# A hybrid attention and state-space block on one core: one z granule earlier, the merge started a quarter earlier, two norms rearranged

## The chip, the cores and the metric

The kernel runs on one core of a Trainium2 chip. The core's engines run side by side, each with its own in-order queue: TensorE (PE, with PEld for its weight loads), VectorE (DVE), ScalarE (ACT), GpSimd (POOL) and SyncE (SP), which here only issues transfers. The metric is the device time of one execution in microseconds, the median of several; lower is better.

## The reference, cut to what matters

One decoder block, 256 positions, width 2048, all float32. An attention branch with a top-64 choice of keys for each query and a state-space (SSD) branch run on the same modulated input; they are merged by gates, projected, added to the residual, and a SwiGLU feed-forward part with a second norm and a final norm follow.

```python
h = rms_norm(x, norm1_g[l]) * (1.0 + sc1) + sh1
proj = h @ w_in            # split: c_q, c_kv, k_idx, w_idx, z, xbc, dt, g_a, g_b
y_a = dsa_branch(...)      # idx_score -> top_k -> 16 heads of attention on the chosen keys
y_b = ssd_branch(z, xbc, ...)          # conv, chunked scan, * silu(z), group rms_norm
merged = sigmoid(g_a) * (y_a @ w_proj_a) + sigmoid(g_b) * (y_b @ w_proj_b)
x = x + g1 * (merged @ w_out)
h = rms_norm(x, norm2_g[l]) * (1.0 + sc2) + sh2
x = x + g2 * ((silu(h @ w_gate) * (h @ w_up)) @ w_down)
return rms_norm(x, final_g)
```

## The kernel before, in words

**Layout.** Activations are kept transposed, 128 channels on the partitions by 256 positions; a product granule is one 128x2048 piece of weights, that is 16 tiles of 128x128. Each granule is a `Job`. SP loads the raw piece (1 MB); `split` turns it into a high part `wh` (ACT, L178) and a low part `wl` (DVE, L179); the job's function then issues the matmuls. Activations are split in the same way into 512 columns (high, low). A product of one tile is two matmuls where the accumulator is 512 wide (`wide`: 512 columns for the high weights, 256 for the low, L202 and L203), and three of 256 columns where it is not (L205 to L207). When an accumulator is full, its `post` is put off to the start of the next job (`flush`).

**Order.** `run_jobs` goes through the list of jobs: it runs the posts put off, then splits the weights of the job two places ahead (`process_to`), then runs the job's `pre` hook, then its function. Generators (index scores and top-k, heads, SSD) advance one step for each tick of a job. All this is the order in which instructions are traced; a planner then lays out each engine's queue by this priority and by modelled readiness, so an instruction of lower priority can fill a modelled gap. Background entries (`add_bg`) are pieces of the modulation matrix that DVE multiplies and adds up (L424, L426).

**Stages.** First the small projections and the modulation (to about 300 us); 8 z granules, during which the 8 steps of index scores and then the top-k run on DVE (L638, L639); 8 pairs of heads with a z granule after each; 4 z granules; 16 granules of proj_a (`add_pa`); 48 granules of the convolution input mixed with the last z granules and the first half of proj_b; the second half of proj_b; 16 granules of the output projection (`add_out`); gate and up; down; the final norm.

**A head** (`head_gen`): logits on PE (L749, L750), bias plus mask on POOL (L753, L754), softmax on DVE and ACT (L759 to L766), transposes on PE (L770).

**The merge.** proj_b sums over 32 tiles in four quarters q of 8 granules, each granule two output rows m; `pb` in SBUF holds the sum (L1007). In the last quarter `merge_load` fetches the stored gates `sg` and the stored attention part `sa` for each m, and `merge` multiplies by the gate on DVE (L1038), adds `sa` on POOL (L1039) and splits the result into `mg` (ACT L250, DVE L251). The first granule of the output projection reads `mg` row by row.

**The second norm** (`norm2`, the `pre` of the first gate granule): the squares of 15 rows are summed on POOL, the last row's square stays apart; `rms_rows` sums over the partitions on PE (L301), takes the square root (L293) and the reciprocal (L294), and spreads the result over the partitions on PE (L312); then for each of 16 rows DVE, ACT and DVE make `h2` (L1087 to L1089). **The final norm** does the same, ACT copies the factor to SBUF (L1250), and DVE and POOL multiply the 16 rows (L1254), stored in 9 transfers (L1255) from the SP and ACT queues.

## Time and profile before

| what | value |
|---|---|
| median of 3 runs | 2051.14 us (2050.96 to 2054.85) |
| the profiled execution | 2048.58 us |
| its span, first to last instruction | 2046.9 us |
| busy: PE, DVE, ACT, POOL | 1999.2, 1460.8, 1049.9, 185.0 us |
| mean granted PE clock | 0.987 of full |

PE is busy for 98% of the span. [...] Times in a timeline are microseconds from the span's start.

### The profile page before, as it was taken

To read this page: it belongs to the slowest core of one execution; us is meant where nothing else is said; L and a number is where in the kernel's file an instruction comes from. 1 tells how busy PE (TensorE), PEld (TensorE's weight loads), DVE (VectorE), ACT (ScalarE), POOL (GpSimd) and SP (SyncE) were. 2 spreads that over 40 slices of the span, in tenths; PEclk is the share of its full clock that TensorE was granted. 3 is DMA by queue.
4 is the path that set the end of the run, shared out by engine and by line. 5 is a ranking of instruction groups with operands and counts; after the bars stand their busy time and mean duration, and the time that the engine had idled before them with its cause. 6 is when DMAs were issued, how large, how long until landed. Compare 5 with 4: busy or idle time off the path is not lost.

```text
span 2046.9 us, 31681 instructions
## 1 busy us (share of the span) xinstructions
PE 1999.2 (98%) x12888; PEld 1786.3 (87%) x12888; DVE 1460.8 (71%) x1819; ACT 1049.9 (51%) x1427; POOL 185.0 (9%) x160
## 2 busy tenths in 40 slices
PE   8999999999999999999999999999999999999997
PEld 6899998899888888889989988888888888888886
DVE  6777787977678888888787855667776555544443
ACT  4655474565346766667664434544444444443432
POOL 0000000220000111110112344000000000000000
PEclk8999999999999999999999999999999999999998
DMA  9887776666887767766666676457775555565552
GB/s 372 330 308 294 277 253 242 232 220 229 292 319 282 252 249 254 260 229 242 224 247 217 235 264 212 164 208 292 264 297 197 188 187 187 200 217 187 187 185 83
DMA packets 100033, 490.17 MB, mean 239 GB/s; under 512 B 10512, under 2 KB 43648, under 8 KB 46384
## 3 DMA queue, kind: packets, MB, share of 16 engines
q1 hardware_dynamic: 98224, 484.10, 65.6%
q0 software_dynamic: 704, 3.15, 0.4%
q8 instruction: 101, 1.65, 0.3%
q10 hardware_dynamic: 960, 0.92, 0.1%
q14 instruction: 44, 0.36, 0.0%
HBM read 473.35 MB, written 17.92 MB: 240 GB/s over the span
## 4 chain that ended last, share of the span: by engine, by line
PE 85%; issue 7%; DVE 4%; ACT 3%; POOL 1%; DMA 1%; DVEq 0%; POOLq 0%; ACTq 0%
PE acc_gu L202 15%; PE acc_dn L202 8%; PE acc_cv L202 8%; PE acc_gu L203 8%; PE acc_dn L203 4%; PE acc_cv L203 4%; PE acc_z L202 4%; PE acc_pa L202 3%; PE acc_out L202 3%; PE cyc L706 2%; PE cyc L704 2%; PE cyc L705 2%; PE acc_pb L205 2%; PE acc_pb L206 2%; PE acc_pb L207 2%
## 5 line engine op out<-in xcount | busy, mean ns | idle before, releaser
L179 DVE TENSOR_TENSOR wl<-raw,wh 128x2048 fp32r<-128x2048 f32 (+1 forms) x316 | 722.1, 2286 | 356.5 <-ACT wh L178 355.8
L178 ACT ACTIVATE wh<-raw 128x2048 fp32r<-128x2048 f32 (+1 forms) x316 | 599.1, 1897 | 371.8 <-PE acc_dn L202 99.8
L202 PE MATMUL acc_gu<-h,wh 128*128 128x512 f32 x1312 | 459.6, 396 | 0.0
L203 PE MATMUL acc_gu<-h,wl 128*128 128x256 f32 x1312 | 367.2, 280 | 0.0
L202 PEld LDWEIGHTS acc_gu<-h,wh 128*128 128x128 f32 x1312 | 246.1, 188 | 58.3
L202 PE MATMUL acc_cv<-h,wh 128*128 128x512 f32 x768 | 277.6, 403 | 0.0
L202 PE MATMUL acc_dn<-ffact,wh 128*128 128x512 f32 x704 | 248.8, 396 | 0.0
L203 PEld LDWEIGHTS acc_gu<-h,wl 128*128 128x128 f32 x1312 | 247.6, 189 | 0.0
L203 PE MATMUL acc_cv<-h,wl 128*128 128x256 f32 x768 | 215.6, 281 | 0.0
L203 PE MATMUL acc_dn<-ffact,wl 128*128 128x256 f32 x704 | 198.5, 282 | 0.0
L202 PE MATMUL acc_z<-h,wh 128*128 128x512 f32 x512 | 183.4, 400 | 0.0
L202 PEld LDWEIGHTS acc_cv<-h,wh 128*128 128x128 f32 x768 | 144.1, 188 | 37.4 <-issue 4.7
L426 DVE SCALAR_TENSOR_TENSOR acc<-raw,cact,acc 128x1024 f32<-128x1024 f32 x120 | 158.5, 1321 | 5.2 <-DMA raw<-in_ada_dram 4.7
L202 PEld LDWEIGHTS acc_dn<-ffact,wh 128*128 128x128 f32 x704 | 132.3, 188 | 32.3
L704 PE MATMUL cyc<-h,wh 128*128 128x256 f32 x512 | 147.9, 289 | 5.1 <-ACT cyc L679 1.8
L706 PE MATMUL cyc<-h,wl 128*128 128x256 f32 x512 | 144.8, 288 | 3.1 <-DVE wl L179 3.1
L705 PE MATMUL cyc<-h,wh 128*128 128x256 f32 x512 | 146.4, 286 | 0.0
L203 PEld LDWEIGHTS acc_cv<-h,wl 128*128 128x128 f32 x768 | 145.1, 189 | 1.0 <-issue 0.5
L205 PE MATMUL acc_pb<-y,wh 128*128 128x256 f32 x512 | 145.1, 283 | 0.0
L203 PE MATMUL acc_z<-h,wl 128*128 128x256 f32 x512 | 143.4, 280 | 0.0
L206 PE MATMUL acc_pb<-y,wh 128*128 128x256 f32 x512 | 142.6, 279 | 0.0
L207 PE MATMUL acc_pb<-y,wl 128*128 128x256 f32 x512 | 142.5, 278 | 0.0
(311 smaller groups left out, 3606.2 us busy)
## 6 DMA issues: line engine op xcount, KB each, us to landing
raw<-in_w_gu_dram SPq DMA_DIRECT2D x88, 1024.0 KB, 4.7
raw<-in_ada_dram SPq DMA_DIRECT2D x75, 1024.0 KB, 5.0
raw<-in_w_ssm_dram SPq DMA_DIRECT2D x48, 1024.0 KB, 4.9
raw<-in_w_dn_dram SPq DMA_DIRECT2D x44, 1024.0 KB, 4.7
raw<-in_w_z_dram SPq DMA_DIRECT2D x32, 1024.0 KB, 5.0
raw<-in_w_pb_dram SPq DMA_DIRECT2D x32, 1024.0 KB, 4.8
raw<-in_w_s_dram SPq DMA_DIRECT2D x27, 1024.0 KB, 6.8
raw<-in_w_pa_dram SPq DMA_DIRECT2D x16, 1024.0 KB, 5.3
```

Source lines behind the costliest of these rows:

```text
L178: act.activation(whf[:, o], raw[:, o], AF.Copy)
L179: dve.tensor_tensor(wlf[:, o], raw[:, o], whf[:, o].bitcast(F32), op=ALU.subtract)
L202: pe.matmul(acc, wh, rhs, start=first, stop=last)
L203: pe.matmul(acc[:, :L], wl, rhs[:, :L], start=False, stop=last, skip_group_check=True)
L205: pe.matmul(acc, wh, rhs[:, :L], start=first, stop=False)
L206: pe.matmul(acc, wh, rhs[:, L:], start=False, stop=False)
L207: pe.matmul(acc, wl, rhs[:, :L], start=False, stop=last)
L426: dve.scalar_tensor_tensor(a, r, cact[:, k : k + 1], a, op0=ALU.mult, op1=ALU.add)
L704: pe.matmul(acc, wh[:, t], h[:, k, :L], start=first, stop=False, skip_group_check=True)
L705: pe.matmul(acc, wh[:, t], h[:, k, L:], start=False, stop=False, skip_group_check=True)
L706: pe.matmul(acc, wl[:, t], h[:, k, :L], start=False, stop=(c == n - 1), skip_group_check=True)
```

## The change

A ninth z granule stands ahead of the first pair of heads, and three instead of four follow the last pair (`ZLEAD`). In the third quarter of proj_b (q = 2) the sum so far is already multiplied by the gate and `sa` is added (`merge_most`); in the last quarter the gate, loaded a second time, multiplies the accumulator and the product is added on DVE, with no POOL step. The last row of the output projection and of down uses a 256-column accumulator (`narrow`), so its post is one DVE instruction. `rms_cols` sums the early squares of both halves first, then the last row's. `norm2` is traced ahead of the split of the weights two places ahead (`first`), with four matmuls ahead of the column sums and four behind the spread whose results nobody reads. At the end DVE multiplies with the factor out of PSUM, POOL with the copy in SBUF; the rows are dealt out anew, POOL's four in two pieces.

```diff
+ZLEAD = 9
-OUTC = ((0, 1), (1, 2), (2, 3), (3, 5), (12, 16), (5, 7), (7, 9), (9, 11), (11, 12))
+OUTC = ((0, 1), (1, 2), (2, 4), (12, 14), (4, 6), (6, 8), (14, 16), (8, 10), (10, 12))
+OUTP = 12
@@ run_jobs
+            if job.first and job.pre:
+                job.pre()
             process_to(jobs[min(i + AHEAD, len(jobs) - 1)].entry)
-            if job.pre:
+            if job.pre and not job.first:
                 job.pre()
@@ product_jobs
-                        if not wide:
+                        if not wide or m in narrow:
                             accs[key, m] = accs[key, m][:, :L]
@@ rms_cols
-        for c in range(2):
-            for i, s in enumerate(sums):
+        for i, s in enumerate(sums):
+            for c in range(2):
                 pe.matmul(
-                    ps[:, c : c + 1], s[:, c * P : c * P + P], ones[:, 0:1], start=(i == 0), stop=(i == len(sums) - 1)
+                    ps[:, c : c + 1], s[:, c * P : c * P + P], ones[:, 0:1],
+                    start=(i == 0 and c == 0), stop=(i == len(sums) - 1), skip_group_check=True,
                 )
@@ add_pb
-            dve.tensor_tensor(pb, acc, pb, op=ALU.add)
-            if q == 3:
-                merge(m, pb)
+            if q < 3:
+                dve.tensor_tensor(pb, acc, pb, op=ALU.add)
+                if q == 2:
+                    merge_most(m, pb)
+            else:
+                merge(m, pb, acc)
@@
-        product_jobs(..., pref=merge_load if q == 3 else None)
+        product_jobs(..., pref=merge_load if q >= 2 else None)
@@ merge_load, merge
         sg = tmp.tile([P, L], F32, tag="zv", name="sgr")
+        nc.sync.dma_start(sg, d_sgb[m])
+        Cc["ld", m] = sg
+
+    def merge_most(m, pb):
+
         sa = tmp.tile([P, L], F32, tag="zt", name="sar")
-        nc.sync.dma_start(sg, d_sgb[m])
         nc.sync.dma_start(sa, d_sa[m])
-        Cc["ld", m] = sg, sa
-
-    def merge(m, pb):
-        sg, sa = Cc.pop(("ld", m))
-        dve.scalar_tensor_tensor(pb, sg, 1.0, pb, op0=ALU.add, op1=ALU.mult)
+        dve.scalar_tensor_tensor(pb, Cc.pop(("ld", m)), 1.0, pb, op0=ALU.add, op1=ALU.mult)
         pool.tensor_tensor(pb, pb, sa, op=ALU.add)
+
+    def merge(m, pb, acc):
+        sg = Cc.pop(("ld", m))
+        dve.scalar_tensor_tensor(sg, sg, 1.0, acc, op0=ALU.add, op1=ALU.mult)
+        dve.tensor_tensor(pb, pb, sg, op=ALU.add)
         split_act(pb, Cc["mg"][:, m])
@@ add_out (add_down alike)
-            dve.scalar_tensor_tensor(x1, acc[:, L:], mods[:, 0, m : m + 1], x1, op0=ALU.mult, op1=ALU.add)
+            if acc.shape[1] > L:
+                dve.scalar_tensor_tensor(x1, acc[:, L:], mods[:, 0, m : m + 1], x1, op0=ALU.mult, op1=ALU.add)
...
+        product_jobs(..., pref=pref, wide=True, narrow=(15,))
@@ norm2
-        r = rms_rows([Cc["acc"], Cc["last"]], D, "n2")
+        dummy = ps_side("busy")
+        for _ in range(4):
+            pe.matmul(dummy[:, :L], ones, Cc["acc"], start=True, stop=True)
+        r = rms_cols([Cc["acc"], Cc["last"]], D, "n2")
+        rp, r = r, rms_all(r, "n2")
+        for _ in range(4):
+            pe.matmul(dummy[:, :L], rp[:, 0:1].to_broadcast([P, P]), Cc["last"], start=True, stop=True)
@@ the list of jobs
-    sp = Spread(8, BG[0])
-    for i in range(8):
+    sp = Spread(ZLEAD, BG[0])
+    for i in range(ZLEAD):
         add_z(next(zs))
...
-    sp = Spread(20, BG[1])
+    sp = Spread(28 - ZLEAD, BG[1])
...
-    for _ in range(4):
+    for _ in range(12 - ZLEAD):
         add_z(next(zs))
@@ the end
-        eng = pool if b == 16 else dve
+        eng, f = (pool, r) if a >= OUTP else (dve, rp)
         v = Fd["x2"][:, a:b]
-        eng.tensor_tensor(v, v, r[:, None, :].to_broadcast([P, b - a, L]), op=ALU.mult)
+        eng.tensor_tensor(v, v, f[:, None, :].to_broadcast([P, b - a, L]), op=ALU.mult)
```

## Rows read from the trace of the kernel before

**Rows 1.** The page's first part: busy time, share of the span and instructions of each engine.

```profile
PE 1999.2 (98%) x12888; PEld 1786.3 (87%) x12888; DVE 1460.8 (71%) x1819; ACT 1049.9 (51%) x1427; POOL 185.0 (9%) x160
```

**Rows 2.** The view of waits of engine PE over the whole span: who waited for whom, us in total, times, longest.

```profile
PE pT L770 <- DVE part L766: 5.0, 3, 2.3
...
PE acc_out L202 <- DVE mg L251: 4.0, 2, 3.4
```

**Rows 3.** The first heads. First two stretches of the view of windows (length, then busy time and count of PE, PEld, DVE, ACT, POOL, then the granted PE clock, DMA share, GB/s); then the timeline of PE and of DVE (start, duration, engine, line, operation, count, and in brackets the idle time before it and its releaser).

```profile
359.00:377.00 18.00, 18.00 (x134) 16.82 (x132) 17.96 (x61) 9.52 (x15) 1.08 (x4) 1.00 0.42 162
...
388.20:394.70 6.50, 4.18 (x21) 3.89 (x20) 6.46 (x14) 3.27 (x12) 0.52 (x1) 0.50 0.75 286
...
384.52 0.28 PE L203 MATMUL acc_z<-h,wl 128*128 128x256 f32 x1
...
391.19 0.69 PE L770 MATMUL pT<-ident,part 128*128 128x128 f32 x2 [2.32 <-DVE part L766]
...
374.11 2.30 DVE L179 TENSOR_TENSOR wl<-raw,wh 128x2048 fp32r<-128x2048 f32 x1
...
390.79 0.34 DVE L766 TENSOR_SCALAR part<-part,mx 128x256 f32<-128x256 f32 x1
```

**Rows 4.** The end of the merge and the first granule of the output projection: timeline of PE, one window as above, timeline of DVE and of SP (its transfers' issues).

```profile
1182.44 0.40 PE L202 MATMUL acc_out<-mg,wh 128*128 128x512 f32 x1
...
1191.82 0.79 PE L202 MATMUL acc_out<-mg,wh 128*128 128x512 f32 x1 [3.38 <-DVE mg L251]
...
1191.80:1196.40 4.60, 4.58 (x14) 3.90 (x15) 1.69 (x4) 1.82 (x2) 0.73 (x1) 0.50 0.79 267
...
1181.57 0.43 DVE L1038 SCALAR_TENSOR_TENSOR pbacc<-sgr,pbacc 128x256 f32<-128x256 f32 x1 [1.80 <-DMA sgr<-d_sgb]
...
1191.35 0.42 DVE L251 TENSOR_TENSOR mg<-pbacc,mg 128x256 fp32r<-128x256 f32 x1
...
1174.54 0.33 SPq L1032 DMA_DIRECT2D sgr<-d_sgb  x1
```

**Rows 5.** The third and the last quarter of proj_b, roughly, in the view of windows; and from the view of the tile y (1100 to 1140 us) the last part of the split of the last SSD group: duration min/median/max, first and last start.

```profile
1092.00:1137.00 45.00, 45.00 (x394) 43.29 (x393) 31.98 (x41) 18.68 (x19) 8.40 (x8) 1.00 0.58 208
1137.00:1182.00 45.00, 43.50 (x371) 43.32 (x370) 38.45 (x52) 17.68 (x19) 21.33 (x12) 1.00 0.74 265
...
L251 DVE TENSOR_TENSOR y<-xc,y x4: 418/420/426, 1131.8 to 1133.8; 128x256 fp32r<-128x256 f32 x4
```

**Rows 6.** Timeline of PE: two instructions 16 tiles (one granule) apart in the output projection, two one tile apart in proj_b.

```profile
1262.22 0.39 PE L202 MATMUL acc_out<-mg,wh 128*128 128x512 f32 x1
...
1267.80 0.40 PE L202 MATMUL acc_out<-mg,wh 128*128 128x512 f32 x1
...
1176.44 0.28 PE L205 MATMUL acc_pb<-y,wh 128*128 128x256 f32 x1
...
1176.79 0.28 PE L205 MATMUL acc_pb<-y,wh 128*128 128x256 f32 x1
```

**Rows 7.** The second norm: timeline of PE, of DVE and of ACT; the last row is a float32 matmul of 256 columns (two passes) in the heads.

```profile
1278.61 0.28 PE L301 MATMUL n<-ones,ssq 128*128 128x1 f32 x2
...
1282.63 1.22 PE L312 MATMUL n2b<-ident,rcol 128*128 128x128 f32 x4 [0.55 <-DVE rcol L294]
1285.69 0.76 PE L202 MATMUL acc_g<-h,wh 128*128 128x512 f32 x1 [1.84 <-DVE h L1089]
...
1289.00 0.40 PE L202 MATMUL acc_g<-h,wh 128*128 128x512 f32 x1
...
1279.97 0.48 DVE L1071 SCALAR_TENSOR_TENSOR pbacc<-acc_out,mods,pbacc 128x256 f32<-128x256 f32 x1
...
1280.79 0.40 ACT L1046 ACTIVATE sqs<-pbacc 128x256 f32<-128x256 f32 x1
...
380.77 0.60 PE L750 MATMUL lg<-part 128*128 128x256 f32 x2
```

**Rows 8.** The final norm: timeline of DVE, PE, ACT, POOL and SP, and from the view of transfers (2030 to 2047 us, 40 slices of 0.425 us) what they moved.

```profile
2032.39 0.48 DVE L1148 SCALAR_TENSOR_TENSOR x<-acc_dn,mods,x 128x256 f32<-128x256 f32 x1 [12.44 <-PE acc_dn L203]
...
2034.20 0.36 PE L301 MATMUL nf<-ones,x 128*128 128x1 f32 x2
2034.42 0.36 PE L301 MATMUL nf<-ones,sqs 128*128 128x1 f32 x2
2035.33 0.71 PE L312 MATMUL nfb<-ident,rcol 128*128 128x128 f32 x4 [0.55 <-DVE rcol L294]
...
2036.08 0.38 ACT L1250 ACTIVATE x<-nfb 128x256 f32<-128x256 f32 x1 [1.00 <-PE nfb L312]
...
2036.84 2.56 DVE L1254 TENSOR_TENSOR x<-x 128x256 f32<-128x256 f32 x1
...
2036.54 2.58 POOL L1254 TENSOR_TENSOR x<-x 128x1024 f32<-128x1024 f32 x1 [15.21 <-ACT x L1250]
...
2036.95 0.34 SPq L1255 DMA_DIRECT2D out_dram<-x  x1
...
GB/s 0 0 0 0 0 0 0 0 0 0 0 0 0 0 0 0 0 0 226 82 0 0 0 70 378 390 386 376 378 390 381 381 386 383 388 335 5 0 0 0
```

**Rows 9.** A DVE instruction with one input in PSUM beside a POOL addition, in the merge: timeline of both.

```profile
1185.95 0.42 DVE L1007 TENSOR_TENSOR pbacc<-acc_pb,pbacc 128x256 f32<-128x256 f32 x1
...
1186.11 0.74 POOL L1039 TENSOR_TENSOR pbacc<-pbacc,sar 128x256 f32<-128x256 f32 x1 [1.32 <-DVE pbacc L1038]
```

More of the change, by code (lines that the diff above doesn't have):

```diff
@@ L166, in __init__ @@
             self.fn, self.pre, self.ticks, self.tk = fn, pre, ticks, tk
+            self.first = False
             self.entry = len(entries)
@@ L209, in hybrid_block_kernel, with product_jobs @@
     accs = {}
-    def product_jobs(key, srcs, order, rhs, post, pre=None, ticks=1, pref=None, wide=False):
+    def product_jobs(key, srcs, order, rhs, post, pre=None, ticks=1, pref=None, wide=False, narrow=()):
         count, seen = {}, {}
@@ L1017, in add_pb @@
         order = [(2 * mp + m, k) for m in range(2) for k in range(8)]
-        product_jobs(f"pb{q}_{mp}", [w_pb[8 * q + mp]], order, rhs, post, pre=pre, ticks=ticks, pref=merge_load if q == 3 else None)
+        product_jobs(f"pb{q}_{mp}", [w_pb[8 * q + mp]], order, rhs, post, pre=pre, ticks=ticks, pref=merge_load if q >= 2 else None)
     Cc = {}
@@ L1073, in post @@
             sum_squares(Cc["p"], x1, m == 0, m == 15, Cc)
-        product_jobs(f"out{m}", [w_out[m]], [(m, k) for k in range(KT)], rhs, post, pref=pref, wide=True)
+        product_jobs(f"out{m}", [w_out[m]], [(m, k) for k in range(KT)], rhs, post, pref=pref, wide=True, narrow=(15,))
     Fd = {}
@@ L1132, in add_gu_first @@
             jobs.append(Job(w_gu[g], body(order[16 * g : 16 * g + 16]), norm2 if g == 0 else None, piece=512 if g == 2 else 2048))
+            jobs[-1].first = g == 0
     def add_gu(i):
@@ L1147, in post @@
             x2 = Fd["x2"][:, m]
-            dve.scalar_tensor_tensor(x2, acc[:, L:], mods[:, 3, m : m + 1], x2, op0=ALU.mult, op1=ALU.add)
+            if acc.shape[1] > L:
+                dve.scalar_tensor_tensor(x2, acc[:, L:], mods[:, 3, m : m + 1], x2, op0=ALU.mult, op1=ALU.add)
             dve.scalar_tensor_tensor(x2, acc[:, :L], mods[:, 3, m : m + 1], x2, op0=ALU.mult, op1=ALU.add)
@@ L1154, in add_down @@
             "dn", [w_dn[g] for g in range(44)], [(m, k) for m in range(16) for k in range(FT)],
-            lambda k: Fd["act"][:, k], post, pref=pref, wide=True,
+            lambda k: Fd["act"][:, k], post, pref=pref, wide=True, narrow=(15,),
         )
```

## The prediction

> **What bounds the kernel now.** The page's first part comes first: PE is busy for 1999.2 of 2046.9 us [rows 1], so no other engine's total counts, and the change issues no less work on PE. What can be gained lies where PE stands still or runs at the lower clock. So the second view is that of the waits of PE: of its entries, two belong to parts the change touches and are long, 5.0 us for the transposes of the first heads and 4.0 us for the merged rows [rows 2]. [...]
>
> *The first heads.* DVE is full in the 18 us before the stall (17.96 us), its last top-k step ends where the split at 374.11 starts, and the last softmax product that the transposes wait for ends at 390.79 + 0.34 = 391.13 us, while PE had come to them at 384.8 [rows 3]. Of the 6.3 us between, PE stands still for 5.0. Then, from 388.2 to 394.7, the clock is at 0.50 (1.2 GHz) and PE is busy for 4.18 us; half of that, 2.1 us, is lost too [rows 3]. Loss here: 7.1 us.
>
> *The merge.* A granule of the output projection takes 1267.80 - 1262.22 = 5.58 us [rows 6], so 16 take 89.3. From the first (1182.44) [rows 4] to the end of the last (1278.61, where the column sum follows it) [rows 7] it is 96.2. Loss: 6.9 us, which is 4.0 us of waiting, the window at clock 0.50 that follows it (4.58 us busy, 2.3 lost) [rows 2, 4] and 0.6 elsewhere. What is late is the last gate: its predecessor was asked for at 1174.54 and used only at 1181.57, 7.0 us later, behind weights in the same queue, and the last `mg` row is worked off one by one until 1191.35 and after [rows 4].
>
> *The second norm.* PE's last product ends at 1278.61; at 1289.00 five tiles of the next stage are done, worth 5 x 0.349 = 1.74 us [rows 6, 7]. Loss: 8.65 us. *The end.* The last accumulator is read at 2032.39, the first store is issued at 2036.95, and the span ends at 2046.9 [rows 8].
>
> **The change part by part.**
>
> *One z granule ahead of the heads.* It puts 5.58 us [rows 6] ahead of the first transposes, which PE then reaches at 384.8 + 5.6 = 390.4. DVE's splits come one for each job in either order, so up to then its queue grows only by the post of a z granule instead of none for a pair: two instructions of 0.42 us (the like in rows 9). The softmax would end at 391.13 + 0.84 = 392.0, leaving some 1.1 us, since the first three quarters are ready sooner; too short a stop, I think, to lower the clock. Gain 7.1 - 1.1 = 6.0. If the planner lets one more split (2.30 us) [rows 3] in between and the clock falls again, 3.9 + 2.1 remain and the gain is 1; at best 7.1. The removed z granule behind the heads was cover of 5.6 us for the last two; three stay, 16.7 us, so I cost that at nothing.
>
> *The merge.* Behind the last product each row now needs two DVE instructions (0.42 each), one on ACT (0.40, as the square in rows 7) and one on DVE (0.42) [rows 4, 9]; for two rows that is some 3.0 us, with a split of 2.30 us in front 5.3: done at 1187.7, and PE wants the last two at 1182.44 + 14 x 0.349 = 1187.3 and 1187.7. POOL, which shares these us with DVE's splits, is out of the chain, and so are the transfers of `sa` that stood between the two gates on SP. Gain 6.9 less 0.7 for a late gate: 6.2. If the gate again needs 7.0 us [rows 4], now asked for one granule ahead (1176.8), the rows come at 1189.1: 1.8 us of waiting and 2.3 of clock stay, gain 2.8. At best 6.9.
>
> *What the third quarter takes over.* 16 gate products of 0.43 us (6.9 us of DVE), 16 POOL additions, 32 transfers on SP; 16 gates are loaded twice. DVE's 31.98 of 45 us become 38.9, as many as the last quarter has now (38.45), and there PE lost 1.5 us [rows 5]. Behind each gate product waiting for its transfer stand, on DVE, the low halves of the weights and the last SSD group, whose last split starts at 1133.8 [rows 5] and is wanted some 2 to 4 us later (128 tiles at 0.353 us and the wait of 1.5, counted back from 1182.44, begin at 1135.7 at the latest, and seven tiles stand before it). About four gate products fall into that chain's last 10 us (1.7 us), and `sa` takes turns with the SSD squares in the same two buffers. I charge 1.4 us, between 0 and 4 (1.7 us, and a wait of 1.80 as in rows 4, rounded up).
>
> *Narrow accumulator.* Three matmuls of 256 columns take 1176.79 - 1176.44 = 0.35 us a tile, two of 512 and 256 take 5.58 / 16 = 0.349 [rows 6]: 60 tiles cost under 0.1 us. It saves one DVE instruction in each chain, 0.52 us from start to start.
>
> *The second norm.* Without the second post instruction (1279.97 + 0.48) and the splits before the square, the square would be there at about 1280 instead of 1281.19 [rows 7]. But the four added matmuls hold PE: one of that kind takes 0.43 us from start to start (busy 0.60) [rows 7], so four end at 1278.61 + 1.72 = 1280.3, and two pairs of column sums follow for each part, 0.22 us a pair [rows 8], to 1281.2. Now the sums end at 1282.07, so 0.85 us is won. The spread took 1.22 us in the second norm and 0.71 in the final norm [rows 7, 8], where the clock stayed up: 0.5 more. From its end to the next product 1.8 us stay, hidden work for the second four (1.72). Then the five slow tiles: 1289.00 - 1285.69 = 3.3 us instead of 1.74, at most 1.5. Sum 2.8. Without the clock, and with a piece of a split in the chain (0.6), 0.3; at best 3.2.
>
> [...] The rows show that each of three long stops was followed by work at 1.2 GHz, and that the final norm's shorter one was not [rows 3, 4, 7, 8]. [...]
>
> *The end.* One post instruction less (0.52), a pair of column sums less (0.22), no ACT copy ahead of DVE (0.42 from 2036.08 to 2036.50): the first store is issued 1.16 us sooner, at 2035.8. Now POOL's piece of 2.58 us holds DVE's second multiplication for 2.56 us, and after the first store (226 GB/s in one slice) the transfers stand still for three slices; 2.1 MB are then moved at some 380 GB/s [rows 8]. With one input in PSUM a DVE instruction kept its 0.42 us beside a POOL addition [rows 9], so DVE should run on, and the transfers be one stretch of 2.1 MB / 380 GB/s = 5.5 us, from 0.7 us behind the first issue (2036.5) to 2042.3 with small gaps, where they now end at 2045.2. Gain 2.9. If POOL still holds DVE, only the 1.16 is sure; if there are no gaps, 3.3.
>
> **Sum.** 6.0 + 6.2 - 1.4 + 2.8 + 2.9 = 16.5 us off the profiled execution's 2048.58 (span 2046.9). The median of the runs shown is 2.56 us above it, at 2051.14; the stages are the same, so I take the gain off the median: **2034.6 us**. All lower bounds together give 1.0 + 2.8 - 4.0 + 0.3 + 1.2 = 1.3 us, all upper ones 20.5 us; the likeliest case holds gains of 12 to 20.5, that is 2030.6 to 2039.
>
> **The rivals.**
> *The stall moves on.* For it: DVE is full up to the heads, and its late work is not taken away. Against it: the added granule brings more PE time than DVE time. Heads 1, the rest as summed but the merge at 4: a gain of 9.3, 2041.8.
> *The clock is not won back*, if the runs behind the median did not lose it at these places: without 2.1, 2.3 and 2.0 us the gain is 10.1, 2041. Against it: all three stops in the trace lost it.
> *No change to be told:* each part at its lower bound, a gain of 1.3, 2049.8. Against it: four parts would have to fail at once.
> *Slower: the third quarter jams.* `sa` waits on SP for POOL to give a buffer back, and the next raw weights stand behind it on SP. Weights are split two granules ahead, so this decides from a hold of about 11 - 4 = 7 us a granule; if each of 8 granules then lost 2.8 us (half of 5.6), 22.4 us go and with the other gains, 17.9, it is 2055.6. For it: a gate took 7.0 us once [rows 4]. Against it: the last quarter now does the same and PE lost 1.5 us there [rows 5].
>
> **Chances.** The sum as forecast 0.65, the stall that moves on 0.18, the clock 0.08, no change 0.05, slower 0.04. About 0.2% (4 us) is what a measurement of this kernel can tell from no change. So faster 0.91, same 0.05, slower 0.04. The range takes the likeliest case and most of the second and third: 2030 to 2043.
>
> **What would show it.** In the profile after: no wait of the transposes for L766 over 1.5 us and PEclk 1.0 around 390 to 400; no wait of `acc_out` for `mg` over 1 us; 16 more gate products and no new PE wait over 2 us before the last quarter; clock 1.0 through the second norm and some 5.7 us instead of 7.1 from PE's last product to the next; POOL's two pieces beside undelayed DVE multiplications, and one stretch of stores. I am wrong if PE waits for the last SSD group's `y`, if DVE's multiplication out of PSUM still takes over 2 us, or if the first pair still stops PE by 4 us.

## The result and the profile after

Median 2041.43 us (7 runs, 2038.45 to 2048.57) against 2051.45 us of the kernel before in the same series (7 runs, 2050.85 to 2058.73): ratio 0.9943, 95% interval 0.9929 to 0.9957, so 8.8 to 14.6 us faster, 11.7 by the ratio. The forecast was 16.5 us: its time of 2034.6 us lies below every timed run, its range of 2030 to 2043 holds the median.

The profiled execution of the changed kernel is the longest of its seven, 2048.57 us with a span of 2046.9: to a tenth the span of the profiled execution before. Whoever compares the two spans sees no change. The stages have to be compared. The table gives, for the runs of this study, when the first z product starts and how long each stage lasts (from the first weight load of one accumulator tile to that of the next; the last to the end of the span). "Merge" is the output projection with the second norm and the first gate products, up to the first product of the stage of gate and up. The labels are those of the experiments below.

| run | z starts | heads | proj_a, conv | proj_b | merge | gate, up | down, end | span |
|---|---|---|---|---|---|---|---|---|
| before | 304.6 | 202.9 | 331.6 | 343.2 | 138.1 | 462.9 | 263.6 | 2046.9 |
| after | 306.1 | 200.7 | 334.0 | 346.6 | 130.8 | 467.1 | 261.6 | 2046.9 |
| whole_again | 305.6 | 200.8 | 332.9 | 344.0 | 131.1 | 462.9 | 261.5 | 2038.8 |
| heads_only | 304.6 | 200.6 | 333.5 | 343.4 | 140.7 | 462.9 | 263.5 | 2049.2 |
| merge_only | 304.8 | 203.0 | 334.7 | 346.6 | 134.6 | 467.2 | 263.5 | 2054.4 |
| norms_only | 305.6 | 203.0 | 334.9 | 346.4 | 131.4 | 464.6 | 261.7 | 2047.6 |
| bg_out | 304.2 | 198.7 | 334.6 | 341.4 | 130.1 | 464.6 | 261.6 | 2035.2 |
| lead_ten | 305.1 | 196.7 | 334.9 | 345.1 | 130.8 | 467.1 | 261.5 | 2041.2 |
| no_busy | 304.5 | 200.5 | 332.7 | 342.9 | 131.8 | 462.9 | 261.6 | 2036.9 |
| end_two | 303.7 | 200.6 | 333.2 | 350.0 | 130.3 | 462.9 | 261.7 | 2042.4 |
| all_copy | 306.1 | 200.7 | 332.7 | 342.0 | 132.1 | 467.2 | 261.9 | 2042.7 |
| quarter | 305.0 | 200.5 | 333.3 | 345.0 | 130.4 | 464.6 | 262.1 | 2040.9 |
| best | 305.9 | 202.1 | 338.4 | 343.5 | 129.8 | 464.6 | 261.6 | 2045.9 |
| best_end | 303.8 | 202.3 | 334.5 | 346.1 | 131.0 | 467.1 | 261.3 | 2046.1 |

Two kinds of columns. Heads and "down, end" repeat to some tenths: 202.9 to 203.0 us with eight granules ahead, 200.5 to 200.8 with nine; 263.5 or 263.6 with the old end, 261.5 to 261.7 with the new one (262.1 in the run `quarter`, where the last broadcast took 1.22 us instead of 0.71). The others move by themselves: gate and up, whose code is the same in all runs, takes 462.9, 464.6 or 467.1 us, and the kernel after takes 467.1 in one execution and 462.9 in another. The merge column moves too: `heads_only` has the code of the kernel before there, and takes 140.7 us instead of 138.1. So the 7.3 us that the merge column gained in the first trace, with 2.2 in the heads and 2.0 at the end, were hidden by 1.5 us at the start, 2.4, 3.4 and 4.2 us in stages where the change has no or little part.

The differences give what the change is worth: heads 2.3, end 2.0, and for the merge column 7.4 or 10.0, counted from 138.1 (`before`) or from 140.7 (`heads_only`) down to 130.7, the mean of the nine runs that have both its parts and the extra matmuls. In all that is 11.7 or 14.3 us, less what the third quarter of proj_b costs; the ratio says 11.7. The proj_b column scatters too much (341.4 to 350.0) to tell that cost; the waits of PE tell more (see the merge's last quarter).

**The heads after.** View of waits of PE, then the timeline of DVE and PE, then one window.

```profile
PE pT L776 <- DVE part L772: 2.0, 2, 1.6
...
369.50 2.28 DVE L182 TENSOR_TENSOR wl<-raw,wh 128x2048 fp32r<-128x2048 f32 x1
371.70 0.42 DVE L252 TENSOR_TENSOR zs<-acc_z,ev 128x256 f32<-128x256 f32 x1
...
372.63 0.41 DVE L743 SCALAR_TENSOR_TENSOR zt<-zt,zs 128x256 f32<-128x256 f32 x1
...
378.25 1.27 DVE L432 SCALAR_TENSOR_TENSOR acc<-raw,cact,acc 128x1024 f32<-128x1024 f32 x1
...
379.83 1.28 DVE L432 SCALAR_TENSOR_TENSOR acc<-raw,cact,acc 128x1024 f32<-128x1024 f32 x1
...
390.83 1.48 DVE L432 SCALAR_TENSOR_TENSOR acc<-raw,cact,acc 128x1024 f32<-128x1024 f32 x1
...
392.37 1.62 DVE L432 SCALAR_TENSOR_TENSOR acc<-raw,cact,acc 128x1024 f32<-128x1024 f32 x1
393.91 1.68 DVE L772 TENSOR_SCALAR part<-part,mx 128x128 f32<-128x128 f32 x4
...
394.44 0.33 PE L776 MATMUL pT<-ident,part 128*128 128x128 f32 x1 [1.55 <-DVE part L772]
...
393.80:400.50 6.70, 5.53 (x30) 4.93 (x31) 6.70 (x18) 4.11 (x10) 1.18 (x2) 0.75 0.88 342
```

PE still stops, 2.0 instead of 5.0 us [rows 2], and the clock still falls behind it (0.75 in the last row). PE came later as forecast; but so did DVE. Ahead of the scaling at 393.91 stand the moved granule's split (369.50) in the middle of the top-k, its evacuation and gate (371.70, 372.63), and two pairs of background accumulations (378.25 and 379.83; 390.83 and 392.37), where the kernel before had one.

**The merge's last quarter.** The two quarters of [rows 5] in windows, then DVE's gate products that waited for a transfer, and the wait of PE that came of it.

```profile
1092.00:1137.00 45.00, 44.97 (x391) 43.08 (x390) 35.70 (x48) 16.60 (x17) 30.63 (x21) 1.00 0.81 280
1137.00:1187.00 50.00, 48.45 (x397) 48.07 (x396) 39.80 (x62) 20.23 (x22) 4.87 (x3) 0.97 0.80 280
...
1168.66 0.82 DVE L1052 SCALAR_TENSOR_TENSOR sgr<-sgr,acc_pb 128x256 f32<-128x256 f32 x2 [0.98 <-DMA sgr<-d_sgb]
...
1181.68 0.42 DVE L1052 SCALAR_TENSOR_TENSOR sgr<-sgr,acc_pb 128x256 f32<-128x256 f32 x1 [1.87 <-DMA sgr<-d_sgb]
...
PE acc_pb L210 <- DVE sgr L1052: 1.0, 1, 1.0
```

The wait of `acc_out` for `mg` (4.0 us in [rows 2]) is gone from the list. Its place takes a small one, 1.0 us: the accumulator is now given back by the gate product, and that waits for the gate's reload. In this trace the third quarter passes without a stop of PE (44.97 of 45 us). Not in every one: of the eleven traces with the new third quarter, five show PE waiting there for the norm of the last SSD group, by 1.3 (`merge_only`, `no_busy`), 1.6 (`best_end`), 1.8 (`quarter`) and 3.7 us (`end_two`), 0.9 us on the mean of the eleven. In the three traces with the old third quarter PE does not wait there. The longest, from the waits of PE in `end_two`:

```profile
PE ynb L318 <- DVE rcol L299: 3.7, 1, 3.7
```

**The second norm after.** Timeline of PE and two windows.

```profile
1278.09 0.28 PE L212 MATMUL acc_out<-mg,wl 128*128 128x256 f32 x1
...
1278.21 1.89 PE L1100 MATMUL busy<-ssq,ones 128*128 128x256 f32 x8
...
1281.72 0.71 PE L318 MATMUL n2b<-ident,rcol 128*128 128x128 f32 x4 [0.84 <-DVE rcol L299]
1282.27 1.89 PE L1104 MATMUL busy<-sqs,rcol 128*128 128x256 f32 x8
...
1284.28 0.47 PE L207 MATMUL acc_g<-h,wh 128*128 128x512 f32 x1
...
1278.20:1284.30 6.10, 5.14 (x31) 4.32 (x29) 4.97 (x11) 4.06 (x9) 0.00 (x0) 1.00 0.76 259
1284.30:1290.00 5.70, 5.70 (x32) 4.95 (x33) 5.70 (x16) 2.62 (x6) 0.00 (x0) 1.00 0.25 103
```

The granted clock stays at 1.00 through the norm and into the gate products; before it was not [rows 7]. From the last product to the next there are 6.07 us (5.7 forecast, 7.1 before).

**The end after.** Timelines of ACT, DVE and the queues, and what the transfers moved (2030 to 2047 us, as in [rows 8]).

```profile
2037.33 0.38 ACT L1273 ACTIVATE x<-nfb 128x256 f32<-128x256 f32 x1 [1.00 <-PE nfb L318]
2039.09 2.22 ACTq L1278 DMA_DIRECT2D out_dram<-x  x4
...
2037.74 3.74 DVE L1277 TENSOR_TENSOR x<-x,nfb 128x256 f32<-128x256 f32 x7 [1.22 <-ACT x L1273]
...
2038.19 5.08 SPq L1278 DMA_DIRECT2D out_dram<-x  x5
...
GB/s 0 0 0 0 0 0 0 0 0 0 0 0 0 0 0 0 0 0 0 0 0 253 56 123 388 381 234 386 362 383 386 383 386 383 383 386 65 0 0 0
```

DVE is no longer held by POOL (its multiplications of 256 columns take 0.42 us, where one took 2.56 before [rows 8]), but its first multiplication starts at 2037.74, behind ACT's copy, not beside it. The three empty slices of [rows 8] behind the first store have become two thin ones, and a third, three slices later, is little more than half full.

### The profile page after: what moved, and what is told of

Same layout as the page of the kernel before. It is cut to its first block, busy times and chain, and to the rows that moved or that the text cites. A ratio compares the mean times of both kernels' runs of the same rounds, so it can differ in the third digit from the quotient of the medians.

```text
span 2046.9 us, 31891 instructions
## 1 busy us (share of the span) xinstructions
PE 2011.2 (98%) x12964; PEld 1794.5 (88%) x12964; DVE 1458.3 (71%) x1832; ACT 1048.8 (51%) x1427; POOL 187.0 (9%) x161
## 4 chain that ended last, share of the span: by engine, by line
PE 91%; DVE 4%; DMA 2%; ACT 1%; issue 1%; POOL 0%; SPq 0%; DVEq 0%; POOLq 0%; ACTq 0%
PE acc_gu L207 15%; PE acc_cv L207 9%; PE acc_gu L208 8%; PE acc_dn L207 8%; PE acc_z L207 6%; PE acc_cv L208 4%; PE acc_dn L208 4%; PE acc_pa L207 3%; PE acc_z L208 3%; PE cyc L712 3%; PE cyc L710 3%; PE acc_out L207 3%; PE cyc L711 3%; PE acc_pa L208 2%; PE acc_pb L210 1%; PE acc_pb L212 1%
## 5 line engine op out<-in xcount | busy, mean ns | idle before, releaser
L207 PE MATMUL acc_dn<-ffact,wh 128*128 128x512 f32 x660 | 233.2, 396 | 0.0
L208 PE MATMUL acc_dn<-ffact,wl 128*128 128x256 f32 x660 | 186.1, 282 | 0.0
L207 PEld LDWEIGHTS acc_dn<-ffact,wh 128*128 128x128 f32 x660 | 124.0, 188 | 29.9
```

What stands on the lines that cost most here:

```text
L207: pe.matmul(acc, wh, rhs, start=first, stop=last)
L208: pe.matmul(acc[:, :L], wl, rhs[:, :L], start=False, stop=last, skip_group_check=True)
```

## The experiments

**Parts and whole.** The changed kernel once more, and the kernel before with one part each: the granule (`ZLEAD` alone), the merge (`merge_load`, `merge_most`, `merge`), the norms and the end (the rest of the diff).

> The changed kernel once more, to have a second trace of it. Theory A (the parts add up, and the first profiled execution was slowed by chance: its tile pitch in the gate stage and three stretches at 1.2 GHz behind runs of 16 one-column matmuls): the median is 10 to 12 us below before, and this trace need not have the slow stretches at the same places. Theory B (the change itself slows PE's stream): this trace shows them again at the same places, and a pitch of 0.356 us a tile in the gate stage as in the first.

> The kernel before with only the ninth z granule ahead of the heads. Theory A (from the trace after: top-k itself ends 5.8 us later, because DVE's other work fills the added time, so most of the stop stays): 3 us faster, a stop of 2 to 3 us at the first transposes. The prediction's step (DVE's work up to there does not grow): 6 us faster, a stop of about 1 us.

> The kernel before with only the merge begun in the third quarter. Theory A: 4.5 us faster, made of 6.5 won in the first output granule and 2 lost in the last quarter of proj_b, where PE waits for an accumulator that is only given back once the reloaded gate is there. The prediction's step: 4.8 us faster, with the 1.4 us lost in the third quarter and none in the last.

> The kernel before with everything but these two parts: narrow accumulators, the second norm, the final norm and the stores. Theory A (trace after): 2.6 us at the second norm and 2.0 at the end, 4.6 us faster. The prediction's steps: 2.8 and 2.9, 5.7 us faster. If the narrow accumulators cost PE time, 60 tiles would show a pitch above 0.353 us in the last row's 16 and 44 tiles.

Against 29 runs of before: whole 0.9943 (0.9927 to 0.9959); granule 0.9987 (0.9975 to 0.9999), 2.7 us; merge 0.9979 (0.9963 to 0.9994), 4.3 us; norms and end 0.998 (0.9969 to 0.9992), 4.1 us. The parts add up to 11.1 us against 11.7. So theory A of the repeated run stands, and B falls: the repeated run's gate stage took 462.9 us, as before. Of the prediction's three amounts the intervals leave 4.8 (merge) and 5.7 (norms) open, but not 6.0 for the granule (0.2 to 5.1 us). The trace of the merge alone does not show what was expected of it, a wait for the accumulator in the last quarter; PE stops for the SSD group in the third quarter instead (1.3 us).

What differs between two executions of the same kernel in gate and up stands in the view by line and form, 1400 to 1560 us (columns: operation xcount, busy us, mean ns); first the kernel after, then its repetition:

```profile
L207 PE MATMUL acc_gu<-h,wh 128*128 128x512 f32 x444 | 157.2, 399 | 0.0
L208 PE MATMUL acc_gu<-h,wl 128*128 128x256 f32 x444 | 124.7, 281 | 0.0
```

```profile
L207 PE MATMUL acc_gu<-h,wh 128*128 128x512 f32 x451 | 157.0, 394 | 0.0
L208 PE MATMUL acc_gu<-h,wl 128*128 128x256 f32 x451 | 125.6, 278 | 0.0
```

In 160 us without a wait one execution does 451 tiles and the other 444, both at a granted clock of 1.00. The repeated run is not at one speed itself: the matmuls of 512 columns take 391 ns from 1330 to 1430 us and 399 from 1600 to 1760, where the first run takes 399 too. No view shows why.

**The heads: is it DVE's queue?** Once the background entries are dealt out otherwise, once a tenth granule goes ahead.

```diff
-BG = (4, 8, 8, 24, 4)
+BG = (6, 6, 8, 24, 4)      # bg_out
-ZLEAD = 9
+ZLEAD = 10                 # lead_ten
```

> The changed kernel with six of the twelve background accumulations of this stretch in the nine granules ahead of the heads (four before) and six behind, so that the first ones behind come later; the lead stays nine granules. In the repeated run of the changed kernel two pairs of background accumulations (1.26 + 1.27 us and 1.48 + 1.62 us) stand on DVE between the start of the top-k and the first head's scaling at 393.44, and PE waits 1.6 us for that scaling. Theory A, the moved granule took DVE's work along, so DVE sets the end of this stretch: with one pair less, the scaling starts about 390.3, PE's waits for pT fall from 2.0 to under 0.4 us, the clock stays at 2.4 GHz behind it, and the stretch from the first z product to the first pa product is 197 to 198.5 instead of 200.8 us. Rival B, DVE is not the limit but the lead of PE is short, or the scheduler fills the gap with other work: scaling within 1 us of 393.4, wait 1 to 1.6, stretch 200 to 201 us.

> The changed kernel with ten granules of z ahead of the heads instead of nine, nothing else. By the prediction's step a moved granule (16 tiles by 0.35 us) gives 5.6 us of lead and costs DVE nothing ahead of the heads: the scaling stays at about 393.4 and the wait is gone with 4 us to spare. Theory A: the tenth granule takes along its split (2.28 us), its evacuation and gate (0.42 + 0.41 us), and it shifts the background pairs: scaling 2.5 to 6 us later, at 396 to 399.5, with PE there at about 398.5: net lead won 0 to 2.5 us, wait between 0 and 1.6, stretch from z to pa 197.5 to 200.8 us.

Entries: timeline of DVE and PE, and the waits of PE in the heads.

```profile
390.17 2.22 DVE L772 TENSOR_SCALAR part<-part,mx 128x128 f32<-128x128 f32 x4
...
391.82 1.06 PE L776 MATMUL pT<-ident,part 128*128 128x128 f32 x6
...
PE lg L755 <- ACT part L813: 1.7, 1, 1.7
PE acc_q L210 <- DVE mx L765: 0.9, 1, 0.9
```

PE no longer waits for the scaling, the clock stays at 1.00, and the stage is 2.1 us shorter, 198.7. So theory A holds, with two reservations. The scaling starts at 390.17, as foretold (390.3), but 1.5 us of that come from an earlier start of the z products; counted from the first of them it starts at 86.0 instead of 87.8, 1.8 us sooner for a pair of 2.6. And two other waits, 1.7 us at the logits (0.6 in the repeated run) and 0.9, make up for the 2.0 at the transposes: PE waits 2.6 us in all in both. What is won is mostly the clock, 1.00 instead of 0.76 over the 7 us from the first transposes on, about 1.7 us. The tenth granule:

```profile
397.11 1.01 DVE L772 TENSOR_SCALAR part<-part,mx 128x128 f32<-128x128 f32 x4
...
397.85 0.82 PE L776 MATMUL pT<-ident,part 128*128 128x128 f32 x6
```

The scaling moves from 393.44 to 397.11, with the z products starting 0.5 us sooner: one granule, 5.6 us for PE, brings DVE 4.2 us more work ahead of the softmax. The net lead is enough all the same: no stop at the transposes, and 196.7 us, 4.1 less than with nine, 6.2 less than before, and less than the 197.5 to 200.8 expected. In the timings neither shows against the changed kernel's 0.9943 (0.9941 and 0.9942, each about 0.002 to either side).

**The second norm without the eight matmuls.**

```diff
-        for _ in range(4):
-            pe.matmul(dummy[:, :L], ones, Cc["acc"], start=True, stop=True)
...
-        for _ in range(4):
-            pe.matmul(dummy[:, :L], rp[:, 0:1].to_broadcast([P, P]), Cc["last"], start=True, stop=True)
```

> The changed kernel without the eight extra matmuls at the second norm; the narrow last product and the shorter chain stay. If the extra matmuls hold the clock (the prediction's step): the granted clock falls to 1.2 GHz in the norm, the broadcast takes 1.22 us instead of 0.71 as in the kernel before, the last out product to the first gate product is 0.5 to 1 us longer than 6.05, and the first 3 us of gate products run at half clock (another 1.4 us): the stretch from there to the first pair of the merged gate stage 1.5 to 2.5 us longer in all. Rival: with the chain short the clock doesn't fall anyway: no half-clock stretch, and within 0.3 us of 6.05.

```profile
1271.40 0.50 PE L306 MATMUL n<-ones,ssq 128*128 128x1 f32 x4
...
1274.31 0.71 PE L318 MATMUL n2b<-ident,rcol 128*128 128x128 f32 x4 [0.71 <-DVE rcol L299]
1276.86 0.77 PE L207 MATMUL acc_g<-h,wh 128*128 128x512 f32 x1 [1.84 <-DVE h L1105]
...
1271.40:1276.80 5.40, 1.81 (x14) 1.45 (x12) 4.90 (x11) 3.98 (x9) 0.00 (x0) 0.84 0.69 235
1276.80:1281.00 4.20, 4.14 (x13) 3.59 (x14) 4.20 (x12) 2.09 (x6) 0.00 (x0) 0.50 0.52 218
```

Without them the chain is shorter, 5.46 us from the last product to the next instead of 6.07 in the repeated run; the broadcast still takes 0.71, not the 1.22 expected. But the clock falls behind it, 0.50 in the last row, and the first gate products, up to the stage of gate and up, take 35.7 instead of 33.4 us. From the end of the output projection to that stage it is 41.0 us against 39.3: in this trace the eight matmuls cost about 0.6 us in the chain, give 2.3 back by the clock behind it, and so are worth 1.7. The time does not tell the kernel without them from the changed one (0.9942, 0.992 to 0.9965).

**The end.** Once the broadcast is made twice (one bank for DVE, one for ACT), and POOL's pieces are stored from SP, which moves the first of them one place back; once DVE too multiplies with the copy.

```diff
-OUTC = ((0, 1), (1, 2), (2, 4), (12, 14), (4, 6), ...)
+OUTC = ((0, 1), (1, 2), (2, 4), (4, 6), (12, 14), ...)          # end_two
...
-    rp = rms_rows([Fd["acc"], Fd["last"]], D, "nf")
+    rc = rms_cols([Fd["acc"], Fd["last"]], D, "nf")
+    rp = rms_all(rc, "nf")
-    act.activation(r, rp, AF.Copy)
+    act.activation(r, rms_all(rc, "nfc"), AF.Copy)          # end_two
-        eng, f = (pool, r) if a >= OUTP else (dve, rp)
+        eng, f = (pool, r) if a >= OUTP else (dve, r)        # all_copy
```

> The changed kernel with the broadcast of the final norm made twice, in two banks: DVE reads one, ACT copies the other; and POOL's two pieces are stored from SP's queue, so that ACT's queue waits for DVE's pieces alone. If DVE's first multiplication stands behind ACT's copy only because both read one bank: it starts 0.7 to 0.8 us behind the start of the broadcast instead of 1.16, the first store 0.4 us earlier, ACT's queue issues its first store under 1.6 us behind the broadcast's start instead of 2.5, the stores run in one stretch near 380 GB/s, and the last down product to the end is 11.5 to 12 instead of 12.7 us. Rival, DVE waits for the copy for another reason: first multiplication still at 1.16 (or later, behind the second broadcast), end within 0.3 us of 12.7.

> The changed kernel with DVE's seven final multiplications reading the copy in SBUF, as POOL's two do, instead of the broadcast in PSUM; nothing else. If the broadcast in PSUM is what keeps DVE from being held by POOL (the prediction's step): the seven multiplications take 5 to 6 us instead of 3.74, those beside POOL's pieces 0.8 us or more longer each than the rest, and the last down product to the end is 13.5 to 14.5 instead of 12.7 us. Rival, the pieces' new order and size made the gain: 3.7 to 4.1 us, end within 0.3 us of 12.7.

In the run with two broadcasts the first of them took 1.19 us; a broadcast takes 0.71 at a granted clock of 1.00 (kernel after, 2036.0 to 2037.5 us) and 1.22 at 0.50 (kernel before, second norm, 1282.6 to 1283.9 us), so by estimate the clock was at about half there too. From the last down product to the end it took 12.7 us, as the changed kernel does, not the 11.5 to 12 expected. In the last version of this study the same end has the 0.71; timeline of PE, DVE and ACT:

```profile
2036.07 0.71 PE L318 MATMUL nfb<-ident,rcol 128*128 128x128 f32 x4 [0.55 <-DVE rcol L299]
...
2036.82 3.74 DVE L1285 TENSOR_TENSOR x<-x,nfb 128x256 f32<-128x256 f32 x7 [0.80 <-PE nfb L318]
...
2037.27 0.38 ACT L1281 ACTIVATE x<-nfcb 128x256 f32<-128x256 f32 x1 [1.45 <-PE nfcb L318]
```

With a bank of its own DVE starts 0.75 us behind the start of the broadcast and waits 0.80 us for PE; with a shared one 1.16, and waits 1.22 us for ACT. So the wait for ACT comes with the bank that both read, and the prediction's "no ACT copy ahead of DVE" overlooked that. Why the two reads stand one behind the other, no run shows. The whole end is 0.3 us shorter (261.3) than in the same version without it (261.6), by one trace of each; the new queue of POOL's pieces is part of that.

With the copy for all, DVE in the view by line and form; the same rows of the repeated run of the changed kernel below it:

```profile
L1277 DVE TENSOR_TENSOR x<-x 128x512 f32<-128x512 f32 x5 | 4.2, 892 | 0.0
...
L1277 DVE TENSOR_TENSOR x<-x 128x256 f32<-128x256 f32 x2 | 1.8, 956 | 1.2 <-ACT x L1273 1.2
```

```profile
L1277 DVE TENSOR_TENSOR x<-x,nfb 128x512 f32<-128x512 f32 x5 | 3.1, 680 | 0.0
...
L1277 DVE TENSOR_TENSOR x<-x,nfb 128x256 f32<-128x256 f32 x2 | 0.8, 418 | 1.2 <-ACT x L1273 1.2
```

As foretold, DVE then takes 5.90 us instead of 3.74, all of it in the two multiplications beside POOL's pieces: reading the factor out of PSUM is what frees it from POOL. But the end is only 0.2 to 0.4 us longer (261.9), not the 0.8 to 1.8 foretold. DVE is done 3.6 us before the span's end, in the repeated run 5.35 (2033.45 to 2038.8): the stores are what ends last, and of DVE's 2.2 us all but 0.2 to 0.4 were to spare. So most of what is won behind the first store goes with the rival's reason, POOL's smaller pieces and their new order.

**The reload of the gate, and all together.**

```diff
+        if "mg" in Cc:
+            sg = Cc["p"].tile([P, L], F32, tag="sgr", name="sgr", bufs=4)
+        else:
             sg = tmp.tile([P, L], F32, tag="zv", name="sgr")
+    def load_ahead(m):
+        for j in range(0 if m == 0 else m + 2, min(m + 3, 16)):
+            merge_load(j)
...
-        product_jobs(..., pref=merge_load if q >= 2 else None)
+        product_jobs(..., pref=merge_load if q == 2 else load_ahead if q == 3 else None)
```

> The changed kernel with the gate's reload of the last quarter of proj_b in four buffers of its own, asked for two products ahead instead of at the product itself. Theory A, the new wait of PE on the gate product comes from the late reload: the waits of acc_pb for sgr (0.9 to 1.0 us in the runs of the changed kernel) and of the gate product for the reload's transfer (10.2 us in 7 waits in the repeated run) are gone, acc_out no longer waits over 0.5 us for mg, and the last quarter from its first product to the first out product is 1 to 2 us shorter. Rival, the DVE queue itself is late there: wait of 0.5 us or more stays though no gate product waits for a transfer.

> The changed kernel with ten granules ahead of the heads, six background entries ahead of them and six behind, and the gate's reload of the last quarter in four buffers two products ahead. From the runs with one of these each: heads 195.5 to 197 us from the first z product to the first pa product (196.7 with ten granules, 198.7 with the entries alone, 200.8 without), no wait for the gate product in the last quarter; in all 4 to 6 us less than the changed kernel's median beside the kernel before, so a ratio of 0.991 to 0.993. Rival: the heads' next wait (attention values on ACT) takes most of it: 199 us or more, ratio 0.994.

> The version with ten granules, entries ahead and early reloads, and with it the broadcast of the final norm in two banks and POOL's pieces stored from SP's queue. Without a drop of the clock at the end (which the one run of that end had, its broadcast took 1.19 us instead of 0.71): DVE's first multiplication 0.72 to 0.8 us behind the start of the broadcast, last down product to the end 12.2 to 12.5 instead of 12.7 us. If the two more products of the broadcast themselves cost that time: again 12.7 to 13.0. In all no difference from the version without it that a timing shows.

With four buffers PE's wait for the gate product is gone, that of `acc_out` is 0.2 us, and from 1130 us on the gate products wait for a transfer 1.1 us in all instead of 10.2. That fits theory A but does not show it: of the eight traces with the late reload only three have a wait for the gate product (1.0, 0.9 and 0.5 us), so one trace without it says little. Proj_b took 345.0 us, inside what it takes anyway, and whether 1 to 2 us were won stays open.

Put together the version is not better: 0.9963 (0.995 to 0.9976) without and 0.9954 (0.9938 to 0.997) with the two broadcasts, and the heads take 202.1 and 202.3 us, nearly as long as before. The forecast (195.5 to 197 us, 0.991 to 0.993) failed; the rival's 199 us or more came true, but not by the wait on ACT that it named. The timeline of PE and a window of the version without them show why:

```profile
402.48 3.14 PE L436 MATMUL ada<-ones,acc 128*128 128x1 f32 x16 [2.68 <-DVE mx L765]
...
404.00:412.00 8.00, 8.00 (x47) 8.00 (x47) 4.14 (x11) 2.43 (x10) 0.40 (x1) 0.64 0.82 303
```

Every eighth background entry ends in a run of 16 one-column products on PE. With six entries ahead and ten granules this run comes 3.5 us behind the first transposes; PE waits 2.7 us for DVE there, and the clock is at 0.64 from 404 to 412 us, which costs 2.9 more. Together that is about the 5.4 us by which the heads are longer than with ten granules alone. With six entries and nine granules (`bg_out`) the same run comes 8 us behind the first transposes, without a wait. So each of the two edits shortens the heads alone, and not both together.

## Why the prediction was right in kind and its gain 5 us too high

*The heads, 6.0 forecast, 2.3 measured.* The step that failed is the one on DVE: "up to then its queue grows only by the post of a z granule". PE did come 6.6 us later (counted from the first z product, 80.2 before and 86.8 after). But between the first top-k step and the first scaling DVE did some 5.6 us more than before: the post (0.8, as charged), one more split (2.3), and one more background pair (2.55). So the first scaling came 6.0 us later (81.8 and 87.8), almost as much as PE. The split is not new work, it only changed its place: before, it stood between the third scaling and the fourth (timeline of DVE, kernel before), and after, ahead of all four.

```profile
388.04 2.83 DVE L179 TENSOR_TENSOR wl<-raw,wh 128x2048 fp32r<-128x2048 f32 x1
```

The end of the fourth scaling, by which the forecast reckoned, moved by 3.0 us (86.5 to 89.5) instead of 0.84, and the pair is most of that. The pair was not thought of at all: dealing 12 entries over 9 and 19 places instead of 8 and 20 moves them. The remaining stop was put at 1.1 us and thought too short to lower the clock; it was 2.0 us, and the clock fell (0.76 over the 7 us from the first transposes on). The prediction had much of this as its lower bound (one more split, the clock falls again, gain 1) and as the first rival, "the stall moves on", with 2041.8. The heads came out nearer to that rival than to the forecast. That its time agrees with the median is luck in part: its sum is another one, with the merge lower than it came out.

*The merge, 6.2.* The output projection up to its last product took 96.3 us before and 97.5 in `heads_only`, which has the same merge; with the new merge it took 90.6 to 92.2 us in eleven traces. `heads_only` is the one to compare with, because its matmuls ran at the same speed there as those of the changed kernel (396 ns for 512 columns on the mean from 1200 to 1270 us, 393 in the kernel before). By it 6.6 us were won in the first trace and 5.6 in the repeated one, which still waits 1.0 us at the first `mg` rows: the forecast was right. Behind the product the prediction counted the time until the rows are ready, but not that the next product needs the same accumulator; that cost 1.0, 0.9 and 0.5 us in three traces. The stop does not always stand where it was found, either: in `norms_only`, which has the old merge, it is 1.1 us instead of 4.0 and the projection takes 92.2 us, but there the clock had fallen just ahead of it (0.51 from 1174 to 1181 us).

*The third quarter, -1.4.* In the first trace it cost nothing. But the prediction's own sign of being wrong, PE waiting for the last SSD group, came true in five of eleven traces, by 1.3 to 3.7 us, and 0.9 on the mean of all eleven. So a charge of 1.4 between 0 and 4 was about right, and the quarter did not jam.

*The second norm, 2.8.* From the last product to the stage of gate and up it took 41.8 us before, and 43.3 and 43.8 in `heads_only` and `merge_only`, which have the same norm; with the new one 39.3 or 39.9. So 1.9 to 4.5 were won, which holds the forecast. The three with the old norm differ by the clock: 0.72, 0.60 and 0.59 over the 12 us from the last product on, 1.00 in the repeated run of the changed kernel. The reason was right too: without the extra matmuls 1.7 of it was lost in the one trace of it.

*The narrow accumulators* were charged at nothing, which no view contradicts.

*The end, 2.9 forecast, 2.0 measured.* The first store comes 0.74 us sooner after the last accumulator is read (3.82 instead of 4.56), not 1.16: the 0.42 for "no ACT copy ahead of DVE" was not won, because DVE waited 1.22 us for ACT's copy out of the same bank. From the first store to the end 8.7 instead of 9.95 us, where a nearly gapless stretch was forecast (6.5 us and the 1.7 behind it, 8.2): the stores start thinly, and ACT's queue issues its first one only at 2039.09, behind POOL's first piece. And DVE's freedom from POOL, which the forecast gave as the reason, makes only 0.4 of these 1.3 us: with the copy for all it is still 9.0.

*The clock.* The traces give the granted clock as a share of full speed, and no view has a figure in GHz; the "1.2 GHz" of the prediction and of the expectations stands for shares like the 0.50 of [rows 3, 4]. The forecast took it as won back where the stop is gone, and the runs agree: 1.00 behind the heads where PE does not stop at the transposes (`bg_out`, `lead_ten`). In all seven traces with nine granules and a stop of 2.0 us there, the granted clock is 0.76 over the 7 us from the first transposes on; in the three with eight granules and stops of 4.7 to 5.0 us it is 0.56 to 0.58. So at this place equal stops lowered the clock equally; behind the old norm it differed from trace to trace (0.72, 0.60, 0.59), and elsewhere (next section but one) the traces differ in whether it fell at all. The second rival, that the old kernel may not lose the clock at these places, is borne out by no trace at the heads and the norm.

*The sum.* The 16.5 us were more than the 11.7 of the ratio by 4.8. Of that 3.7 lie in the heads and 0.9 at the end; merge and norm (9.0 forecast, 7.4 or 10.0 measured) and the third quarter (1.4 and 0.9) agree within their scatter. The forecast also left out how much the other stages vary from one execution to the next.

## What to carry to other kernels

Work that is moved ahead of a stop to give one engine a lead takes along its work on the other engines: count what the late engine does between its own start and the point that is waited for, the background entries that are dealt out by position included, and ask which of it changes its place. Compare traces stage by stage, with several traces of the old kernel as well as of the new one: two spans of 2046.9 us hid a gain of 11.7, and one trace of before alone put the gain of the merge 1 us too low. When DVE and ACT both read one result in PSUM, a second copy of it in another bank lets DVE start without waiting for ACT (0.75 instead of 1.16 us here), which is worth little where transfers end last anyway.

## What was not expected of the hardware

An uninterrupted stream of the same matmuls ran at two speeds, 391 and 399 ns for one of 512 columns, with no wait and a granted clock of 1.00 in both. The repeated run of the changed kernel went from the one to the other within gate and up; the first run had the slower one throughout, and that is 4.2 us from one execution to another. The cause stays open. And the clock falls not only behind stops. In the changed kernel's first trace it fell three times behind a run of 16 one-column products, twice with no wait ahead; timeline of PE for the first of them, and a window behind each:

```profile
807.38 1.93 PE L436 MATMUL ada<-ones,acc 128*128 128x1 f32 x16
...
810.30:813.50 3.20, 3.20 (x14) 2.74 (x13) 3.05 (x5) 3.02 (x8) 0.00 (x0) 0.60 0.31 105
977.70:980.90 3.20, 3.20 (x20) 2.66 (x20) 2.08 (x2) 0.00 (x0) 0.00 (x0) 0.63 0.22 37
1174.60:1178.00 3.40, 3.40 (x18) 3.40 (x18) 3.40 (x7) 0.75 (x2) 0.00 (x0) 0.51 0.97 361
```

PE is busy in every one of them, at 0.51 to 0.63 of the clock. The kernel before has the same three runs, and behind them its trace shows 1.00 each time. So this too is scatter between executions, and part of the 2.4 and 3.4 us by which the stages around them came out longer in that trace.
